# Keys and values by a seven-product (Strassen) form in a two-layer decoder on one core

## The chip, the core and the metric

One core of a Trainium2 chip runs the whole program. Its engines are TensorE (PE: matmuls, with its weight loads beside it), VectorE (DVE), ScalarE (ACT), GpSimd (POOL) and SyncE (SP); each takes its instructions in the order in which they stand in its own queue, and waits at semaphores for the others. Weights come from memory by DMA: SP issues to the hardware queue, POOL to the software queue. A transfer of the software queue can add to what lies at its target ("accumulating transfer"). The metric is the device time of one execution in microseconds, the median of the runs.

## The reference

Two layers over 512 rows of width 1024, in float32. What matters here:

```python
h = rmsnorm(x, norm1_w) * (1 + sc1) + sh1          # sc, sh, g from c @ w_ada
u = h @ w_in                                       # pool, conv, b, c, q, k, v, gate logits
q = apply_partial_rope(rmsnorm(q, q_norm_w), cos, sin)      # by heads of 64; k likewise
o = moba_attention(q, k, v)                        # blocks of 256
merged = (g[0] * (y_pool @ p_pool) + g[1] * (y_conv @ p_conv) + g[2] * (y_attn @ p_attn))
x = x + g1 * (merged @ w_out)
h2 = rmsnorm(x, norm2_w) * (1 + sc2) + sh2
x = x + g2 * ((silu(h2 @ w_gate) * (h2 @ w_up)) @ w_down)
```

`k` and `v` are each 512 columns of `w_in`, so keys and values together are one product of h (512 x 1024) with a 1024 x 1024 matrix.

## The kernel before

Activations lie with features on the 128 partitions: h is eight tiles `big` of 128x512. Every float32 product is made of three (`mm3`): a number is split into a high half, rounded to the matmul's type, and the low half that is left, and high x high, low x high and high x low are added up in PSUM. So all weights need a high half `whi` and a low half `wlo`.

Weights come as a fixed list of chunks, each of eight 128x128 blocks (128x1024, 512 KB). `next_w()` hands out the next chunk and keeps up to four loaded ahead of it. A chunk is fetched by SP into one of three tiles `raw`; `split_w` then writes the high half on ACT (L328) and the low half on DVE (L331), as `raw - whi`. `split_by_transfer` is another way, for the gate columns from 20 on: ACT writes the high half (L339) and its negative into `wlo` (L341), and POOL issues an accumulating transfer that adds the weights on top (L343). There are five tiles each for `whi` and `wlo`.

A Tile scheduler sets the order of instructions, but whatever is wrapped in `pin` or goes through `matmul` stays in the order in which the program names it. Small work on DVE and ACT (pooling steps, convolution, rotary tables, modulation dots) is put on a list `bulk`; each tile of matmuls lets some of it through, at a rate `bulk_rate`, and `flush_bulk()` empties it. Attention runs as a generator (`fibers`) between the matmuls that follow, with a delay counted in the same ticks.

A layer's first part runs so:

1. Eight chunks with four query blocks and three feature columns (the q stage).
2. Feature columns 6, 3 and 7 (24 matmuls of 128x512 each); the pooling chain 0, in layer 0 the rotary tables (`rotary`, L458) and both convolution chains go through `bulk` here.
3. Keys, then values, by `wide()`: 4 chunks of 24 matmuls 128x512 each, for all four groups of 128 rows. Eight dots for the gains G1 (a 512 KB tile of modulation weights each; `ada_dot`, L399) go on here.
4. Feature columns 4 and 5; then, for each of eight output tiles, two gate columns with the pool and conv projections, while attention runs between.
5. GATE2: the attention gates, and the merge of all three branches, whose result `merged` is split again for the output product.

The output product, the second normalisation and the feed-forward follow. Pairs of feed-forward tiles already use a product of seven forms (`GateUp`, `glu_pair`): with halves of the inner dimension and of the rows, the forms are named B21, B11, R1, -V, B22, T3 and T4.

Of the kernel before, what the change touches and what calls it, by code (L numbers as in the profile page):

```python
# [57 lines left out]
NCOL = 74  # L58

# [20 lines left out]
def hybrid_trunk(ctx, tc, xT, ws, ada, cols, pool_w, qk_w, crow, pos, con, out):  # L80
# [210 lines left out]

    def feed_forward():
# [18 lines left out]
    for l in range(L):  # L311
        first_part = [b for b in _plan() if b[0][0] not in ("gate", "up", "down")]
        for blocks in first_part + list(feed_forward()):
            if isinstance(blocks, int):
                pair = GateUp(l, blocks)
                items += [(pair, sub) for sub in range(pair.SUBS)]
            else:
                items.append((None, (l, blocks)))
# [15 lines left out]


# [95 lines left out]
    def ada_step(l, part, j, early):  # L431
        aw = wp.tile([P, D], F32, tag="raw", name=nm("raw"), bufs=RAW) if early else w4([P, D])
        nc.sync.dma_start(aw, ada[l, part, j])
        with tc.issue_after(dots_after[0].ins) if dots_after[0] is not None else nullcontext():
            ins = ada_dot(aw, l, part, j)
        pin(ins)
# [9 lines left out]
    def ada_tasks(l, parts, early=False):  # L446
        out = []
        for part in parts:
            for j in range(KT):
                out.append((1.2, lambda part=part, j=j: ada_step(l, part, j, early)))  # L450
            out.append((0.2, lambda part=part: ada_end(l, part)))
        return out
# [26 lines left out]
    class Norm:  # L479
        def __init__(self, one=False):  # L480
# [7 lines left out]
            self.lo = [bigt() for _ in range(KT)]  # L488

# [43 lines left out]
        def apply(self, l, i, k, lo, hi):  # L533
# [14 lines left out]
            if i == 1:  # L548
                A.activation(self.h[k][:, lo:hi], t[:, lo:hi], AF.Identity, bias=sh)
# [11 lines left out]
        def first_lo(self, k):  # L561
            pin(V.scalar_tensor_tensor(self.lo[k], self.t, mod[0][:, SH1, k:k + 1], f32(self.hi[k]),  # L562
                                       op0=ALU.add, op1=ALU.subtract))

# [42 lines left out]
    def qk_evac(which, qk, ss, t, src):  # L607
        A.activation(qk[t][:, which], src.rearrange("p (h d) -> p h d", d=HD), AF.Copy)
        sq = tmp()
# [221 lines left out]
    for l in range(L):  # L831
# [47 lines left out]
        def wide():  # L879


            pr = ps_pair()
            groups = [ps_mm(), ps_mm(), pr[:, 0], pr[:, 1]]
            for c in range(4):
                w = next_w()
                order = [(kk, t) for kk in range(2) for t in range(TT)]
                for kk, t in sorted(order, key=lambda o: o[1]) if c == 3 else order:
                    k = 2 * c + kk
                    mm3(groups[t], cut(norm.k(k), slice(None), slice(t * P, (t + 1) * P)),
                        wrow(w, 4 * kk), k == 0, k == KT - 1)  # L890
            return groups
# [54 lines left out]

        bulk_rate[0] = 1.4
# [3 lines left out]
        bulk.append((0.4, pool_weights))  # L951
        if l == 0:
            bulk.append((2.0, rotary))
        pool1 = bigt(F32)
        A.activation(pool1, f_ps[1], AF.Copy)
        for j in range(2):
            if j == 1:
                pu = ps_mm()
                feature_tile(pu, next_w())
                uc[1] = bigt(F32)  # L960
# [3 lines left out]
            flush_bulk()  # L964
            z = bigt(F32)
            V.tensor_mul(z, pc, uc[j])
            conv_chain(j, z)
            if j == 1:
                bulk.append((0, lambda: pool_chain(1, pool1)))

        gains = ada_tasks(l, (G1,))
        bulk.extend(gains[:4])
        k_ps = wide()
        for t in range(TT):
            qk_evac(1, qk, ss, t, k_ps[t])
        flush_bulk()
        y_pool, y_conv = [], []
        wc, wsn = rope_tables(l)
        rs = []
        nrq, prq = sm([P, TT, HEADS], tag="nrq", bufs=2), sm([P, TT, HEADS], tag="nrq", bufs=2)  # L980

# [9 lines left out]
        bulk.append((1.6, rstds))  # L991
        for t in range(TT):
# [61 lines left out]
        for step, j in GATE2:  # L1054
# [3 lines left out]
            if j == 0:  # L1058
                drain()
# [327 lines left out]
```

## Time and profile before

| | |
|---|---|
| three runs | 1447.68, 1445.1, 1442.31 us; median 1445.1 |
| profiled execution | 1442.24 us, of which the span of the trace is 1440.5 |
| busy in the span | PE 1433.7, DVE 1014.5, ACT 714.0, POOL 145.7 us |
| moved by DMA | 241.83 MB, mean 168 GB/s |

The times in rows of the profile are microseconds from the start of the span. A row of the timeline has start, duration, engine, line, operation and tiles; square brackets at its end hold idle time of the engine just before it and what ended it. A row of groups has the number of instructions, the total busy time with the mean in nanoseconds of one, and the idle time before. Matmuls are pipelined: each row's duration is longer than the distance to the next one's start.

### The profile page before, as it was taken

What the parts mean: (1) busy time and instruction counts of PE and PEld (TensorE: products, weight loads), DVE (VectorE), ACT (ScalarE), POOL (GpSimd) and SP (SyncE); (2) the same over time, 40 slices, a digit from 0 to 9 for tenths busy, and PEclk for the clock granted to TensorE, in tenths of its full rate; (3) what the DMA queues carried; (4) which work ended last, traced back from release to release, by engine and by line L of the source; (5) the groups of instructions that cost most, each with busy time, mean ns of one, the idle gap of its engine ahead of it and who ended that gap; (6) DMA issues with size and microseconds to landing.
All of it is one profiled execution on the core that took longest, in us unless ns stands there. A gap on an engine that the chain in (4) does not pass through costs nothing.

```text
span 1440.5 us, 21954 instructions
## 1 busy us (share of the span) xinstructions
PE 1433.7 (100%) x8346; PEld 1261.7 (88%) x8346; DVE 1014.5 (70%) x1858; ACT 714.0 (50%) x1199; POOL 145.7 (10%) x204
## 2 busy tenths in 40 slices
PE   9999999999999999999999999999999999999999
PEld 7888888888988998999988888888889989999997
DVE  8887777649686867677798766654578747657663
ACT  5645666733653452535444466666336625525450
POOL 0000110101100311210000000011020102111200
PEclk9999999999999999999999999999999999999999
DMA  9647876665347766756536565567372537637532
GB/s 351 216 149 209 220 184 168 181 229 163 90 140 223 187 179 206 190 146 198 189 125 207 177 146 135 135 154 194 129 208 85 136 114 180 173 105 187 136 88 85
DMA packets 91049, 241.83 MB, mean 168 GB/s; under 512 B 11576, under 2 KB 24256, under 8 KB 90944
## 3 DMA queue, kind: packets, MB, share of 16 engines
q1 hardware_dynamic: 67312, 177.37, 36.8%
q0 software_dynamic: 23040, 62.93, 22.3%
q8 instruction: 65, 1.06, 0.3%
q14 instruction: 40, 0.33, 0.1%
q10 hardware_dynamic: 592, 0.14, 0.0%
HBM read 238.30 MB, written 2.10 MB: 167 GB/s over the span
## 4 chain that ended last, share of the span: by engine, by line
PE 96%; issue 1%; DMA 1%; DVE 1%; ACT 0%; ACTq 0%; DVEq 0%; POOLq 0%
PE mm L151 83%; PE pair L151 12%; PE mm L157 1%; DMA wlo<-in_ws 1%; DMA colt<-in_cols 0%; DVE big L788 0%; DVE big L795 0%; DVE big L562 0%; ACT whi L339 0%; DVE w L399 0%; ACT big L1028 0%; DVE wlo L331 0%; ACT big L575 0%; DVE tmp L555 0%; ACT big L559 0%
## 5 line engine op out<-in xcount | busy, mean ns | idle before, releaser
L151 PE MATMUL mm<-big,whi 128*128 128x512 f32 (+1 forms) x4350 | 1078.0, 339 | 1.0 <-ACT big L1028 1.0
L151 PEld LDWEIGHTS mm<-big,whi 128*128 128x128 f32 x4350 | 744.3, 190 | 87.8 <-issue 2.6
L151 PE MATMUL mm<-big,wlo 128*128 128x512 f32 (+1 forms) x2175 | 735.3, 338 | 0.1
L151 PEld LDWEIGHTS mm<-big,wlo 128*128 128x128 f32 x2175 | 412.6, 190 | 45.3 <-DMA wlo<-in_ws 0.5
L328 ACT ACTIVATE whi<-raw 128x1024 fp32r<-128x1024 f32 (+2 forms) x192 | 198.2, 1034 | 223.2 <-PE mm L151 116.8
L331 DVE TENSOR_TENSOR wlo<-raw,whi 128x1024 fp32r<-128x1024 f32 (+2 forms) x192 | 225.8, 1187 | 53.1 <-ACT whi L328 52.6
L328 ACT ACTIVATE whi<-w 128x1024 fp32r<-128x1024 f32 x72 | 76.2, 1058 | 139.5 <-PE mm L151 85.8
L1073 DVE SCALAR_TENSOR_TENSOR x<-mm,mod,x 128x512 f32<-128x512 f32 (+1 forms) x89 | 61.6, 694 | 75.2 <-PE mm L151 75.0
L399 DVE SCALAR_TENSOR_TENSOR w<-w,csil 128x1024 f32<-128x1024 f32 x80 | 95.9, 1221 | 17.8 <-DMA w<-in_ada 17.7
L331 DVE TENSOR_TENSOR wlo<-w,whi 128x1024 fp32r<-128x1024 f32 x72 | 86.8, 1221 | 28.8 <-ACT whi L328 28.1
L257 POOL DMA_DIRECT2D w<-in_ws x72 | 47.2, 673 | 465.1 <-DVE wlo L331 214.4
L343 POOL DMA_DIRECT2D wlo<-in_ws x48 | 41.0, 855 | 438.1 <-ACT wlo L341 241.5
L259 POOL DMA_DIRECT2D w<-in_ws x72 | 63.4, 906 | 159.0 <-DMA w<-in_ws 155.3
L151 PE MATMUL pair<-whi,big 128*128 128x512 f32 x224 | 76.7, 389 | 0.0
L339 ACT ACTIVATE whi<-raw 128x1024 fp32r<-128x1024 f32 x48 | 51.0, 1063 | 49.4 <-PE mm L151 32.1
L151 PE MATMUL pair<-big,whi 128*128 128x256 f32 (+1 forms) x376 | 74.0, 294 | 0.0
L151 PEld LDWEIGHTS pair<-big,whi 128*128 128x128 f32 x376 | 60.4, 191 | 2.2
L151 PE MATMUL mm<-whi,big 128*128 128x512 f32 x160 | 56.9, 392 | 0.6 <-ACT big L559 0.4
L1033 DVE SCALAR_TENSOR_TENSOR big<-big,mm 128x512 f32<-128x512 f32 x48 | 32.8, 684 | 33.1 <-PE mm L151 31.8
L151 PE MATMUL pair<-big,wlo 128*128 128x256 f32 (+1 forms) x188 | 55.3, 294 | 0.0
L341 ACT ACTIVATE wlo<-whi 128x1024 fp32r<-128x1024 f32 x48 | 50.8, 1059 | 0.3
L151 PEld LDWEIGHTS pair<-whi,big 128*128 128x128 f32 x224 | 42.1, 188 | 8.6
(212 smaller groups left out, 1349.3 us busy)
## 6 DMA issues: line engine op xcount, KB each, us to landing
raw<-in_ws SPq DMA_DIRECT2D x146, 512.0 KB, 4.4
w<-in_ada SPq DMA_DIRECT2D x80, 512.0 KB, 5.5
w<-in_ws POOLq DMA_DIRECT2D x144, 256.0 KB, 4.7
wlo<-in_ws POOLq DMA_DIRECT2D x48, 512.0 KB, 6.8
raw<-in_ws SPq DMA_DIRECT2D x64, 256.0 KB, 4.1
raw<-in_ws SPq DMA_DIRECT2D x24, 384.0 KB, 3.6
raw<-in_ada SPq DMA_DIRECT2D x16, 512.0 KB, 4.4
raw<-in_ws SPq DMA_DIRECT2D x16, 448.0 KB, 5.5
```

Of the source, the lines that this page charges most:

```text
L151: tc.keep_in_program_order(T.matmul(*a, **k))
L157: tc.keep_in_program_order(T.transpose(*a))
L257: nc.gpsimd.dma_start(dst, self.source(0, 1))
L259: nc.gpsimd.dma_start(dst, self.source(*other), accum_op=ALU.add)
L328: A.activation(hi[:, :n], raw[:, :n], AF.Copy)
L331: ins = V.tensor_sub(lo[:, :n], raw[:, :n], f32(hi)[:, :n])
L339: A.activation(hi[:, :n], raw[:, :n], AF.Copy)
L341: A.activation(lo[:, :n], f32(hi)[:, :n], AF.Copy, scale=-1.0)
L343: nc.gpsimd.dma_start(lo[:, i:i + m].rearrange("p b n -> p (b n)"), src, accum_op=ALU.add)
L399: return V.scalar_tensor_tensor(aw, aw, 1.0, csil, op0=ALU.mult, op1=ALU.mult, accum_out=mod[l][:, part, j:j + 1])
L1033: V.scalar_tensor_tensor(sg, sg, 1.0, branch, op0=ALU.add, op1=ALU.mult)
L1073: V.scalar_tensor_tensor(x[k][:, lo:hi], src, mod[l][:, part, k:k + 1], x[k][:, lo:hi], op0=ALU.mult, op1=ALU.add)
```

## The change

Keys and values become one product with seven forms, in both layers. The weights' quarters are named by `(kk, z)`, with `kk` the half of the inner dimension and `z` 0 for the keys, 1 for the values: B11 and B21 are the two halves for the keys, B12 and B22 those for the values. The rows of h are halved too (`early`, `late`: rows 0-255 and 256-511). A class `KeyValue` makes 14 chunks (7 forms, 2 chunks each):

- chunks 0 to 3 (B21, B11) are fetched raw; their low halves come by accumulating transfer;
- chunks 4 to 9 come from two tiles `x`: POOL copies one quarter into each and adds another by accumulating transfer, ahead of time; DVE adds a raw quarter of 128x1024 between the forms, and `split_w` makes the halves;
- chunks 10 and 11 come from four tiles of 128x512 (`far`), filled in the same way by POOL (`summed_rows`) and split row by row (`split_rows`);
- chunks 12 and 13 are fetched raw and split by ACT and DVE.

On the side of h, `sums_one` and `sums_two` make the sums of row halves on DVE and split them; the first norm keeps eight whole tiles `h` for this. Keys and values are put together from the PSUM groups with copies on ACT and additions on DVE. Each chunk now serves 12 matmuls of 128x512: 168 in a layer where there were 192.

Also moved: `rotary()` from the `bulk` list to right behind the q stage; the convolution chains, the second pooling chain and the pooling weights to behind the values, where three gate columns now stand first (the list of chunks is reordered by `AFTER_KEYS`); the eight G1 dots from the K/V stage to GATE2; the loads for layer 0's SC2/SH2 dots run one ahead of their dots.

```diff
+KEYS = 12
+AFTER_KEYS = (20, 28, 21, 4, 5, 29)
...
+        def summed(self, tile, other, cp):
+            flat = tile.rearrange("p b n -> p (b n)")
+            nc.gpsimd.dma_start(flat, self.source(0, 1, cp))
+            nc.gpsimd.dma_start(flat, self.source(other[0], other[1], cp), accum_op=ALU.add)
...
+        def load(self, sub):
+            form, cp = divmod(sub, 2)
+            if sub == 0:
+                self.near, self.far = [None] * 2, [None] * 2
+            if sub == 2:
+                self.x = [w4([P, C_BLOCKS, P]) for _ in range(2)]
+                for i in range(2):
+                    self.summed(self.x[i], (1, 1), i)
+            if form < 2:
+                kk = 1 - form
+                raw = self.raw(kk, 0, cp)
+                if form == 1:
+                    self.near[cp] = raw
+                return split_by_transfer(raw, self.l, self.blocks(kk, 0, cp))
+            if form in (2, 3):
+                w = split_w(self.x[cp], C_BLOCKS)
+                pin(V.tensor_add(self.x[cp], self.x[cp], self.near[cp]))
+                if form == 2:
+                    self.near[cp] = self.raw(1, 0, cp)
+                    self.far[cp] = [bigt(F32) for _ in range(2)]
+                    self.summed_rows(self.far[cp], (0, 0), cp)
+                return w
+            if form == 4:
+                return split_w(self.x[cp], C_BLOCKS)
+            if form == 5:
+                return split_rows(self.far[cp])
+            return split_w(self.raw(1, 1, cp), C_BLOCKS)
...
+        def keys_values(qk, ss, made, tables, then):
...
+            for _ in form(e, "B21", True):
+                pass
+            for _ in form(a, "B11", True):
+                pass
+            for t in range(2):
+                A.activation(qk[t][:, 1], heads(a[t]), AF.Copy)
+                V.tensor_add(qk[t][:, 1], qk[t][:, 1], heads(e[t]))
+                squares(1, ss, t, qk[t][:, 1].rearrange("p h d -> p (h d)"))
+            for cp in form(c, "R1", True):
+                two[cp] = sums_two(cp, *made[cp][:2])
...
+            for cp in form(a, "-V", False):
...
+            for _ in form(c, "B22", False):
...
+            for _ in form(a, "T3", False):
...
+            for cp in form(d, "T4", True):
...
+        if l == 0:
+            rotary()
         bulk_rate[0] = 1.4
         pool_chain(0, f_ps[0])
...
-        if l == 0:
-            bulk.append((2.0, rotary))
...
-        gains = ada_tasks(l, (G1,))
-        bulk.extend(gains[:4])
-        k_ps = wide()
...
-        fibers.append([3, attention(l, qk, v, nrq, prq, y_attn)])
+        fibers.append([5, attention(l, qk, v, nrq, prq, y_attn)])
+        bulk.append((0.4, pool_weights))
+        for j in range(2):
+            conv_chain(j, zs[j])
+        pool_chain(1, pool1)
+        bulk_rate[0] = 1.6
+        ready = [gate() for _ in range(3)]
+        flush_bulk()
...
             if j == 0:
                 drain()
+                late = len(bulk)
+                bulk.extendleft(reversed(ada_tasks(l, (G1,))))
+                bulk_rate[0] = 1.3
```

The order of instructions at the places that the prediction speaks of follows. A row has the line, the operation, output and inputs, and the shape. First VectorE in layer 0, behind the q stage, before: the low half `wlo_592` is that of feature column 7, `wlo_598` and `wlo_604` are those of the first two chunks of the keys; L915 to L925 are the pooling chain.

```order
L331 TENSOR_TENSOR wlo_592<-raw_588,whi_590 128x1024
L915 COPY big_618<-big_581 128x1
L920 TENSOR_TENSOR big_618<-big_581 128x511
L331 TENSOR_TENSOR wlo_598<-raw_594,whi_596 128x1024
L331 TENSOR_TENSOR wlo_604<-raw_600,whi_602 128x1024
L915 COPY big_621<-big_618 128x2
L917 SCALAR_TENSOR_TENSOR big_621<-big_618,cont 128x510
L925 SCALAR_TENSOR_TENSOR tmp_624<-big_621,cont,big_581 128x496
```

The same engine and place, now: `wlo_634` is the low half of column 7; `rope`, `cosc` are the rotary table, L984 to L990 the sums of h's row halves, and L670 their low halves.

```order
L986 SCALAR_TENSOR_TENSOR big_728<-big_729,big_150 128x256
L565 SCALAR_TENSOR_TENSOR rope_615<-rope_612,ang 128x32
L990 SCALAR_TENSOR_TENSOR big_729<-big_728,big_154 128x256
L566 SCALAR_TENSOR_TENSOR rope_615<-rope_612,rope_615 128x32
L567 SCALAR_TENSOR_TENSOR rope_615<-rope_612,rope_615 128x32
L670 TENSOR_TENSOR big_734<-big_728,big_733 128x512
L568 TENSOR_SCALAR rope_615<-rope_615 128x32
L984 TENSOR_TENSOR big_738<-big_155,big_151 128x256
L569 TENSOR_SCALAR rope_615<-rope_615 128x32
L985 TENSOR_TENSOR big_737<-big_151 128x256
L572 COPY cosc<-cosc 128x4x8
L402 TENSOR_TENSOR wlo_634<-raw_630,whi_632 128x1024
```

The low half of column 7 stood ahead of most of the pooling chain and of all of the rotary table, and stands behind both now; the first keys' low halves are gone from this engine.

ScalarE at this place, before: `whi_596`, `whi_602` and `whi_685` are high halves of the keys' first chunks, L572 a high half of the pooling result, L475 the table and the sine.

```order
L328 ACTIVATE whi_596<-raw_594 128x1024
L328 ACTIVATE whi_602<-raw_600 128x1024
L328 ACTIVATE whi_685<-raw_683 128x1024
L572 ACTIVATE big_628<-tmp_624 128x512
L941 ACTIVATE big_701<-big_680,colt 128x512
L328 ACTIVATE whi_722<-raw_720 128x1024
L961 ACTIVATE big_717<-mm_682 128x512
L903 ACTIVATE pwh_650<-tmp_644 128x256
L475 ACT_TABLE_LOAD
L475 ACTIVATE sins<-rope_661 128x4x8
```

And now: `whi_638`, `whi_645`, `whi_699` are the high halves of the keys' first three chunks (L419), L421 the negative copies that the accumulating transfers wait for, L669 high halves of the pooling result and of the sums of h.

```order
L419 ACTIVATE whi_638<-raw_636 128x1024
L419 ACTIVATE whi_645<-raw_643 128x1024
L669 ACTIVATE big_672<-tmp_668 128x512
L571 ACT_TABLE_LOAD
L571 ACTIVATE sins<-rope_604 128x4x8
L419 ACTIVATE whi_699<-raw_697 128x1024
L669 ACTIVATE big_733<-big_728 128x512
L571 ACTIVATE cosc<-rope_615 128x4x8
L421 ACTIVATE wlo_640<-whi_638 128x1024
L421 ACTIVATE wlo_647<-whi_645 128x1024
L421 ACTIVATE wlo_701<-whi_699 128x1024
```

The cosine stands ahead of the first negative copy, and the third high half, with its transfer, ahead of the cosine. On POOL the transfers of this place are, in a row (before, the queue held the pooling weights' clearing and then the gates' low halves):

```order
L314 DMA w_691<-in_ws 128x1024
L314 DMA w_692<-in_ws 128x1024
L315 DMA w_691<-in_ws 128x1024
L315 DMA w_692<-in_ws 128x1024
L423 DMA wlo_640<-in_ws 128x1024
L423 DMA wlo_647<-in_ws 128x1024
L423 DMA wlo_701<-in_ws 128x1024
L423 DMA wlo_753<-in_ws 128x1024
L353 DMA big_821<-in_ws 128x512
L353 DMA big_822<-in_ws 128x512
```

The copies for `x` and what is added to them go first, the four low halves of the first forms next, then the rows for T3.

Last, VectorE in GATE2 of layer 0, before: L1033 and L1067 merge a tile, L573 is its low half, L399 are modulation dots.

```order
L1033 SCALAR_TENSOR_TENSOR big_3161<-big_3161,mm_3291 128x512
L1067 TENSOR_TENSOR big_3161<-big_3161,big_2430 128x512
L1033 SCALAR_TENSOR_TENSOR big_3194<-big_3194,mm_3310 128x512
L1067 TENSOR_TENSOR big_3194<-big_3194,big_2612 128x512
L573 TENSOR_TENSOR big_3307<-big_3161,big_3306 128x512
L573 TENSOR_TENSOR big_3326<-big_3194,big_3325 128x512
L331 TENSOR_TENSOR wlo_3368<-raw_3364,whi_3366 128x1024
L331 TENSOR_TENSOR wlo_3374<-raw_3370,whi_3372 128x1024
L399 SCALAR_TENSOR_TENSOR w_3382,mod_116<-w_3382,csil 128x1024
```

And now the corresponding stretch (L1202 and L1241 merge, L670 is the low half, L479 are dots), a little ahead of the last tiles:

```order
L479 SCALAR_TENSOR_TENSOR w_3236,mod_116<-w_3236,csil 128x1024
L479 SCALAR_TENSOR_TENSOR w_3251,mod_116<-w_3251,csil 128x1024
L402 TENSOR_TENSOR wlo_3267<-raw_3263,whi_3265 128x1024
L479 SCALAR_TENSOR_TENSOR w_3275,mod_116<-w_3275,csil 128x1024
L479 SCALAR_TENSOR_TENSOR w_3290,mod_116<-w_3290,csil 128x1024
L402 TENSOR_TENSOR wlo_3305<-raw_3301,whi_3303 128x1024
L479 SCALAR_TENSOR_TENSOR w_3314,mod_116<-w_3314,csil 128x1024
L1202 SCALAR_TENSOR_TENSOR big_2997<-big_2997,mm_3307 128x512
L1241 TENSOR_TENSOR big_2997<-big_2997,big_1715 128x512
L670 TENSOR_TENSOR big_3326<-big_2997,big_3325 128x512
L479 SCALAR_TENSOR_TENSOR w_3336,mod_116<-w_3336,csil 128x1024
L1202 SCALAR_TENSOR_TENSOR big_3055<-big_3055,mm_3329 128x512
```

Dots that stood behind the merged tiles, or in the K/V stage, stand between them.

More of the change, by code (lines that the diff above doesn't have):

```diff
@@ L290, in load, with __init__, blocks, source @@
             return split_w(raw, C_BLOCKS)
+    class KeyValue:
+        SUBS = 14
+        def __init__(self, l):
+            self.l = l
+        def blocks(self, kk, z, cp):
+            return [("in", kk * HK + 2 * cp + i, KEYS + 4 * z + b) for i in range(2) for b in range(4)]
+        def source(self, kk, z, cp):
+            (_, _, src), = runs(self.l, self.blocks(kk, z, cp))
+            return src
+        def begin(self):
+            pass
[3 more added lines that the diff above has]
+            nc.gpsimd.dma_start(flat, self.source(other[0], other[1], cp), accum_op=ALU.add)
+        def raw(self, kk, z, cp):
+            raw = rawt()
+            fetch(raw, self.l, self.blocks(kk, z, cp))
+            return raw
+        def load(self, sub):
[25 more added lines that the diff above has]
+            return split_w(self.raw(1, 1, cp), C_BLOCKS)
+        def summed_rows(self, tiles, other, cp):
+            for i, tile in enumerate(tiles):
+                c = slice(i * S, (i + 1) * S)
+                nc.gpsimd.dma_start(tile, self.source(0, 1, cp)[:, c])
+                nc.gpsimd.dma_start(tile, self.source(other[0], other[1], cp)[:, c], accum_op=ALU.add)
     def feed_forward():
@@ L332, in split_w, with split_rows @@
         pin(ins)
+        return hi, lo
+    def split_rows(tiles):
+        hi = wp.tile([P, C_BLOCKS, P], F32R, tag="whi", name=nm("whi"), bufs=5)
+        lo = wp.tile([P, C_BLOCKS, P], F32R, tag="wlo", name=nm("wlo"), bufs=5)
+        rows = lambda t, i: t[:, 4 * i:4 * i + 4].rearrange("p b n -> p (b n)")
+        for i, tile in enumerate(tiles):
+            A.activation(rows(hi, i), tile, AF.Copy)
+            pin(V.tensor_sub(rows(lo, i), tile, f32(rows(hi, i))))
         return hi, lo
@@ L446, in ada_tasks, with step @@
     def ada_tasks(l, parts, early=False):
[L447 to L451, printed above, removed]
+        every = [(part, j) for part in parts for j in range(KT)]
+        kept, out = [], []
+        load = lambda n: ada_load(l, *every[n], early, kept)
+        def step(n):
+            if early and n + 1 < len(every):
+                load(n + 1)
+            if not early:
+                load(n)
+            ada_step(l, *every[n], kept)
+        if early:
+            out.append((1.2, lambda: load(0)))
+        for n, (part, j) in enumerate(every):
+            out.append((1.2, lambda n=n: step(n)))
+            if j == KT - 1:
+                out.append((0.2, lambda part=part: ada_end(l, part)))
         return out
@@ L877, in feature_tile, with sums_one @@
                 mm3(o, wblk(w, k), norm.k(k), k == 0, k == KT - 1)
[L879 to L891, printed above, removed]
+        def sums_one(c):
+            h1, h2 = norm.h[c], norm.h[HK + c]
+            one, two = bigt(F32), bigt(F32)
+            r1, nv, t3 = one[:, :BLOCK], one[:, BLOCK:], two[:, :BLOCK]
+            V.tensor_sub(t3, h2[:, BLOCK:], h1[:, BLOCK:])
+            V.tensor_sub(r1, h1[:, :BLOCK], h1[:, BLOCK:])
+            V.scalar_tensor_tensor(nv, t3, -1.0, h1[:, :BLOCK], op0=ALU.mult, op1=ALU.subtract)
+            return one, two, split_from(one)
@@ L1036, in hybrid_trunk @@
         for j in range(KT):
-            s0, s1 = gate(), gate()
+            s0, s1 = [ready.pop(0) if ready else gate() for _ in range(2)]
+            if j == 2:
+                bulk_rate[0] = 0.35
             if j % 2 == 0:
```

129 lines of the change are left out of this document (96 added, 33 removed).

## The prediction

> **What bounds the kernel now.** I read the engine shares first, then the clock slices, the waits of TensorE and the chain that ended last. From the page, and from the waits of TensorE:
>
> ```profile
> span 1440.5 us, 21954 instructions
> PE 1433.7 (100%) x8346; PEld 1261.7 (88%) x8346; DVE 1014.5 (70%) x1858; ACT 714.0 (50%) x1199; POOL 145.7 (10%) x204
> PEclk9999999999999999999999999999999999999999
> ...
> PE pair L151 <- POOL ones L203: 1.1, 1, 1.1
> PE mm L151 <- ACT big L1028: 1.0, 2, 0.5
> PE mm L151 <- ACT big L559: 0.4, 1, 0.4
> PE pair L151 <- ACT ccol L773: 0.3, 1, 0.3
> PE pair L151 <- DVE big L795: 0.2, 1, 0.2
> ```
>
> TensorE (PE) is busy for 1433.7 of 1440.5 us, at a granted clock of 0.9 or more in every slice, and its five waits add up to 3.0 us. The time is the number of matmuls times their pitch. So a removed matmul is paid back in full, unless a wait stands where it stood, and since there are next to no waits now, every wait that the change makes is a loss. The question is therefore whether VectorE (DVE), ScalarE (ACT) and the transfers keep ahead of the shortened products. The pitch, from the chain (start, duration, number), and the place where the keys begin in layer 0, from the timeline (the last matmul of feature column 7 has the weights second, the first of the keys has them first):
>
> ```profile
> 53.76 19.72 PE mm L151 x87
> ...
> 71.73 0.39 PE L151 MATMUL mm<-big,wlo 128*128 128x512 f32 x1
> 71.95 0.39 PE L151 MATMUL mm<-whi,big 128*128 128x512 f32 x1
> ```
>
> 19.72 / 87 = 0.2267 us for a 128x512 matmul. Each lasts 0.39 us but the next starts 0.22 us later, so the pitch, not the duration, is the price. Call T0 = 71.95 the start of the keys; column 7 is 24 matmuls, 5.44 us, and begins at 66.51.
>
> **The matmuls removed.** Keys and values were 8 weight chunks of 24 matmuls in each layer, 192; now they are 14 of 12, 168, all 128x512. 24 x 0.2267 = 5.44 us a layer, 10.88 us in both. The stage shrinks from 43.5 to 38.1 us, and a chunk is used up in 2.72 us instead of 5.44. This is the gain if nothing waits.
>
> **The work that must hide in the stage.** Windows, one for each row: the last columns ahead of the keys and the keys and values, in layer 0 and in layer 1; then, for comparison, one pair of feed-forward tiles, which already uses this kind of product.
>
> ```profile
> 53.80:72.00 18.20, 18.20 (x82) 15.06 (x81) 14.58 (x28) 11.92 (x19) 0.31 (x1) 1.00 0.72 239
> 72.00:115.50 43.50, 43.50 (x194) 36.02 (x193) 35.95 (x90) 17.78 (x26) 1.84 (x2) 1.00 0.51 169
> 763.60:782.00 18.40, 18.40 (x83) 15.24 (x82) 13.36 (x24) 9.31 (x16) 0.31 (x1) 1.00 0.68 214
> 782.00:825.50 43.50, 43.50 (x193) 36.02 (x193) 34.34 (x76) 17.31 (x24) 1.69 (x2) 1.00 0.53 165
> 480.00:497.00 17.00, 17.00 (x144) 17.00 (x143) 14.05 (x20) 9.94 (x16) 5.75 (x9) 1.00 0.87 219
> ...
> q1 hardware_dynamic: 67312, 177.37, 36.8%
> q0 software_dynamic: 23040, 62.93, 22.3%
> ...
> L331 DVE TENSOR_TENSOR wlo<-raw,whi 128x1024 fp32r<-128x1024 f32 (+2 forms) x192 | 225.8, 1187 | 53.1 <-ACT whi L328 52.6
> L399 DVE SCALAR_TENSOR_TENSOR w<-w,csil 128x1024 f32<-128x1024 f32 x80 | 95.9, 1221 | 17.8 <-DMA w<-in_ada 17.7
> L1033 DVE SCALAR_TENSOR_TENSOR big<-big,mm 128x512 f32<-128x512 f32 x48 | 32.8, 684 | 33.1 <-PE mm L151 31.8
> ...
> 67.35 1.53 DVE L943 SCALAR_TENSOR_TENSOR big<-big,colt,big 128x511 f32<-128x511 f32 x2
> 69.94 0.42 DVE L904 TENSOR_TENSOR pwl<-tmp,pwh 128x256 fp32r<-128x256 f32 x1
> ```
>
> Columns after the window are the length, the busy time of PE, weight loads, DVE, ACT and POOL, the clock, the DMA share and GB/s. DVE is busy 35.95 of 43.5 us in the K/V stage of layer 0. The change takes from there the eight gain dots (8 x 1.22 = 9.8 us, row of L399) and the rest of the pooling, convolution and rotary chains (two convolutions of 1.53, some ten steps of about 0.7: 10 us, an estimate), and adds: ten subtractions for low halves of 128x1024 where there were eight (+2.4 us), four additions of 128x1024 (4.9), eight evacuation additions of 512 (5.5), and of the rows' 16 sums of 256 and 8 low halves of 512 about half, the rest lying ahead of the keys (8 x 0.42 + 6 x 0.69 = 7.5). That comes to 36.5 us in 38.1: tight, but the feed-forward window shows DVE at 14.05 of 17 and ACT at 9.94 with PE busy for all of it. I charge nothing inside the stage. ACT gains 8 copies of h a layer in the normalisation ahead (8 x 0.61, the row of L572 below), and evacuations and negative copies in the stage; at 17.78 of 43.5 it covers them. Without that cover each late low half would stop PE for what it is late, up to 1.2 us.
>
> The transfers: a layer's keys and values now fetch 20 pieces of 512 KB where there were 8: 8 by the hardware queue, 12 by the software queue (4 low halves, 8 for two-term sums). The queues' shares above give their rates with all 16 engines at work: 177.37 MB in 0.368 x 1440.5 us is 335 GB/s, 62.93 MB in 0.223 x 1440.5 is 196 GB/s. 8 x 0.524 MB / 335 + 12 x 0.524 / 196 = 12.5 + 32.1 = 44.6 us. That is more than the 38.1 us of the stage, so it must start ahead of it, and it does: the copies for the sums stand behind the last scale and shift dots, which free their tiles (near 47 us, row below), some 25 us ahead of T0.
>
> **Layer 0, just ahead of the keys.** Here the change moves work into a place without slack. Rows of DVE, ACT and the software queue's low halves (L343: what it takes to issue, and how long until it has landed):
>
> ```profile
> 46.82 1.22 DVE L399 SCALAR_TENSOR_TENSOR w<-w,csil 128x1024 f32<-128x1024 f32 x1
> 57.68 1.22 DVE L331 TENSOR_TENSOR wlo<-raw,whi 128x1024 fp32r<-128x1024 f32 x1
> 63.40 1.06 ACT L328 ACTIVATE whi<-raw 128x1024 fp32r<-128x1024 f32 x1 [3.00 <-DMA raw<-in_ws]
> 64.36 0.61 ACT L572 ACTIVATE big<-tmp 128x512 fp32r<-128x512 f32 x1
> 65.01 0.69 DVE L573 TENSOR_TENSOR big<-tmp,big 128x512 fp32r<-128x512 f32 x1 [1.36 <-ACT big L572]
> 68.81 1.28 ACT L475 ACT_TABLE_LOAD   x1
> ...
> L343 POOL DMA_DIRECT2D wlo<-in_ws x48: 835/855/987, 107.3 to 1004.2; - x48
> DMA to landing us min/median/max: 5.2/6.8/11.3
> L341 ACT ACTIVATE wlo<-whi 128x1024 fp32r<-128x1024 f32 x48 | 50.8, 1059 | 0.3
> ```
>
> Column 7's low half is made at 57.68 now, 9 us ahead of its first use (66.51 plus two matmuls, 66.96). In the new order it stands behind the whole rotary table, whose last step waits for ACT; ACT stands there behind the high halves of the keys, and the third of these behind its transfer. That transfer takes the place of the one which ended ACT's idle time at 63.40. Walk: the pooling result and the Sin table load (0.61 and 1.28) keep ACT until about 64.4; high half 1.06, row's high half 0.61, DVE's 0.69, two 256-wide sums (about 0.4 each), the last rotary steps and ACT's cosine (some 0.8 together), then 1.22 for column 7: about 69. PE wants it at 66.96, so it waits 2.0 us. Bounds: 0 if DVE and ACT run a little denser than I walk; 4 if the raw transfers, which the new copies now meet in a stretch that moves 239 GB/s, land 2 us late.
>
> Next in line are the four low halves by transfer. ACT writes the first negative copy (1.06) only behind the cosine, about 67.9 to 69.0; then POOL issues and the data land 6.8 us later (median), 75.8. PE starts the keys at 71.95 + 2.0 and wants it one matmul later, 74.2: 1.6, bounds 0 (landing 5.2) and 5.7 (11.3). I take 1.4, since the wait for column 7 is itself rounded up. The next three come 2.7 us apart at the software queue's 196 GB/s, as fast as PE uses them, so I charge them nothing; 2 us if the hardware queue takes half the engines meanwhile.
>
> A rule of the Trainium skill speaks for less here: "DMA: Bandwidth & Descriptors", section "Anatomy of one DMA — SWDGE (gpsimd) path", fits a transfer of that path as 2.0 us plus the bytes at 436 GB/s, so an estimate of 3.2 us for 512 KB. By it the first low half would be there at about 72.2, the 1.4 us would go and the sum below would be 1437.1. The row's shortest landing, 5.2 us, says that an accumulating transfer amid other traffic is not that fast, so I keep the row.
>
> In layer 1 there is no rotary table and the same four transfers can be issued from about 763, as ACT has 9.31 of 18.4 us busy there: no charge, bound 2 us.
>
> **The first tiles behind the values.** Two convolution chains, the pooling chain and the pooling weights move behind the values; three gate tiles (16.3 us of PE) are placed there to cover them, and their first reader comes behind those and two more columns: nothing, with 1 us as the bound, as POOL's queue now also holds the weights' clearing behind the last transfer.
>
> **The end of the gates.** The gain dots move into the stage where attention's gated sums are merged. Windows of layer 0, and what ends that stage (the last two merged low halves, and PE's first matmul of the output product that is near them):
>
> ```profile
> 302.00:318.00 16.00, 16.00 (x72) 13.27 (x71) 8.64 (x12) 5.30 (x7) 0.00 (x0) 1.00 0.60 212
> 318.00:334.00 16.00, 16.00 (x73) 13.24 (x72) 11.22 (x16) 6.09 (x8) 0.00 (x0) 1.00 0.16 58
> 336.05 1.37 DVE L573 TENSOR_TENSOR big<-big,big 128x512 fp32r<-128x512 f32 x2
> 339.17 0.62 PE L151 MATMUL mm<-big,whi 128*128 128x512 f32 x2
> ```
>
> DVE's 8.64 + 11.22 = 19.9 of 32 us become 29.6 with eight dots, and some layer 0 modulation dots remain besides. The last merged row is ready at 337.4 now and wanted at about 339.2; two or three dots stand ahead of it that were behind it, so it comes near 340: 0.9 us in layer 0, bounds 0 and 2. Layer 1 has no such remaining dots: nothing.
>
> **Sum.** -10.9 + 2.0 + 1.4 + 0.9 = -6.6 us. The profiled execution took 1442.24 us (span 1440.5 and 1.7 around it), 2.9 below the median 1445.1 of the three runs; from it the sum gives 1435.6, from the median 1438.5, and the median is what I forecast against. Half a per cent, about what a measurement of this kernel can tell from no change, is 7.2 us: the line to faster is 1437.9, next to the forecast.
>
> **Rivals.**
> Clean: every wait above is inside my rounding, 10.9 us come through, less at most 1.5: 1434.2 to 1435.7. For it: PE waits only 3.0 us in a kernel whose feed-forward already runs such products without a gap. Against it: 9 us of lead for column 7 is given up in the new order.
>
> Slow train: the four transfers of layer 0 land late and spaced by more than 2.72 us. 5.7 instead of 1.4 for the first and 2 for the others make 6.3 more, half of it 3.2: a net gain of 0.3 to 3.4, so 1441.5 to 1445. For it: the longest landing is 11.3 us. Against it: the median is 6.8.
>
> Slower: the transfers bound both K/V stages. What must arrive by a stage's end is 12.5 us by the hardware queue, 6.3 us for the four weight chunks ahead (4 x 0.524 MB / 335), and 6.29 MB by the software queue, in 38.1 + 25 = 63 us. It breaks the cover when the software queue gets less than 6.29 MB / 44.2 us = 142 GB/s, and eats the whole 5.44 us of a layer below 6.29 / 49.6 = 127 GB/s; at 110 GB/s it loses 13 us a layer, which gives 1445.1 - 10.9 + 26 = 1460. For it: 196 GB/s holds only with the engines to itself. Against it: the feed-forward window moves 219 GB/s by both queues with PE busy throughout.
>
> A rule bears on this: the Trainium skill, same page, section "SWDGE vs HWDGE vs iDMA", says that each engine takes the two paths' queues in turn. That would share, not starve; no run here shows it alone.
>
> **How the numbers follow.** Forecast with waits of 4 us, by one and a half more or less (1436 to 1441): 0.50. Clean: 0.22. Slow train: 0.20. Slower or nearly so (1446 to 1460): 0.08. Faster by over 0.5% is the clean case and a bit under half of the forecast's: 0.45. Slower by over 0.5% is the larger part of the last: 0.05. The rest is the same, 0.50. The range leaves out the last rival and reaches from the clean end to the slow train's: 1433.8 to 1445.5.
>
> **What would show it.** Right: matmuls fall by 48 and their 128x512 pitch stays 0.227; two waits of PE in layer 0, one for column 7's low half near 67 us (by DVE), one for a low half by transfer near 74; layer 1's stage without a wait; DVE near full at the stage where the gains now stand. Wrong: a low half made ahead of 67 us (clean); waits for low halves by transfer in layer 1 too, with landings over 10 us (the rivals with the transfers); or PE waiting for DVE within the stage, which would make DVE, that I cost at nothing there, the bound.

## The result, and the profile after

The changed kernel takes 1458.9 us (median of four runs, 1456.9 to 1460.6) against 1443.8 for the kernel before in the same set: a ratio of 1.010, interval 1.0074 to 1.0126. I forecast 6.6 us less; it is 15 more. From the page of the changed kernel, then TensorE's waits (engine, line, releaser: us in total, times, longest):

```profile
span 1458.9 us, 22095 instructions
PE 1433.4 (98%) x8298; PEld 1254.5 (86%) x8298; DVE 1056.0 (72%) x1938; ACT 757.0 (52%) x1266; POOL 171.4 (12%) x236
PEclk9999999998999999999999999999999999999999
...
PE mm L155 <- DVE wlo L402: 4.3, 1, 4.3
PE mm L155 <- ACT big L669: 3.5, 4, 1.3
PE pair L155 <- DMA wlo<-in_ws: 3.2, 1, 3.2
PE mm L155 <- DMA wlo<-in_ws: 2.9, 2, 1.7
PE mm L155 <- ACT big L844: 1.4, 1, 1.4
PE mm L161 <- DVE big L1202: 1.4, 1, 1.4
```

48 matmuls are gone, yet PE's busy time is what it was (1433.7), and the waits, 3.0 us before, are now over 20. Busy time that should have fallen by 10.9 us points to slower matmuls: one slice of the clock row is an 8, and 13.7 us in two stretches are at half clock, which costs up to 6.8 us. The places come out of one landmark, the same run of 288 matmuls in each layer's feed-forward, in the chain that ended last, before and after (start, duration, number):

```profile
427.08 49.95 PE mm L151 x288
1138.15 49.95 PE mm L151 x288
```

```profile
444.23 49.95 PE mm L155 x288
1156.65 49.95 PE mm L155 x288
```

Layer 0 arrives there 17.15 us late and layer 1 adds 1.35. Since each should have come 5.44 earlier, layer 0 loses 22.6 us and layer 1 6.8, 29.4 in all. Windows of the changed kernel (length, busy time of PE, PEld, DVE, ACT, POOL, then clock, DMA share, GB/s), and layer 0's column 7:

```profile
66.00:72.00 6.00, 1.68 (x7) 1.06 (x7) 5.96 (x21) 4.58 (x7) 0.49 (x1) 1.00 0.26 87
72.10:75.40 3.30, 3.30 (x10) 2.53 (x9) 2.29 (x8) 3.30 (x6) 1.98 (x3) 0.50 0.76 182
340.00:355.00 15.00, 10.79 (x31) 5.92 (x31) 11.77 (x19) 6.53 (x8) 0.00 (x0) 0.78 0.44 144
348.60:358.70 10.10, 7.71 (x16) 4.53 (x16) 8.29 (x12) 4.75 (x6) 0.00 (x0) 0.50 0.49 160
...
71.66 0.51 PE L155 MATMUL mm<-big,wlo 128*128 128x512 f32 x1 [4.32 <-DVE wlo L402]
```

Three losses are large. At the front TensorE waits 4.3 us for column 7's low half and then runs 3.4 us at a granted clock of 0.50, which costs 1.7 more; the keys begin at 78.4 instead of 71.95. At the end of the gates it waits in pieces from 341 to 354, and from 348.5 to 358.7 runs at half clock: 10 us in all, by the distances between matmul starts. In layer 1 it waits 3.2 us for a key's low half and 1.7 for a gate's. Some 6 us of layer 0 are small waits beside attention and at the first gate.

What came as predicted: the keys' and values' stage itself, 38.1 us in layer 0 from its first matmul to its last without a wait, and the pitch.

### The profile page after: what moved, and what is told of

Same layout as the page of the kernel before. It is cut to its first block, busy times and chain, and to the rows that moved or that the text cites. A ratio compares the mean times of both kernels' runs of the same rounds, so it can differ in the third digit from the quotient of the medians.

```text
span 1458.9 us, 22095 instructions
## 1 busy us (share of the span) xinstructions
PE 1433.4 (98%) x8298; PEld 1254.5 (86%) x8298; DVE 1056.0 (72%) x1938; ACT 757.0 (52%) x1266; POOL 171.4 (12%) x236
## 4 chain that ended last, share of the span: by engine, by line
PE 82%; DVE 6%; DMA 6%; ACT 3%; issue 2%; POOL 0%; SPq 0%; ACTq 0%; POOLq 0%; DVEq 0%
PE mm L155 72%; PE pair L155 9%; DMA raw<-in_ws 4%; DMA wlo<-in_ws 2%; PE mm L161 1%; DVE w L479 1%; DVE wlo L402 1%; ACT whi L399 1%; ACT whi L419 1%; DMA x<-in_xT 0%; DVE tmp L651 0%; DVE big L658 0%; DVE raw L479 0%; DVE big L1202 0%; ACT big L669 0%
## 5 line engine op out<-in xcount | busy, mean ns | idle before, releaser
L399 ACT ACTIVATE whi<-raw 128x1024 fp32r<-128x1024 f32 (+2 forms) x180 | 185.1, 1029 | 200.5 <-PE mm L155 103.6
L402 DVE TENSOR_TENSOR wlo<-raw,whi 128x1024 fp32r<-128x1024 f32 (+2 forms) x180 | 211.4, 1184 | 45.0 <-ACT whi L399 44.7
L399 ACT ACTIVATE whi<-w 128x1024 fp32r<-128x1024 f32 x84 | 88.9, 1058 | 156.8 <-PE mm L155 91.9
L402 DVE TENSOR_TENSOR wlo<-w,whi 128x1024 fp32r<-128x1024 f32 x84 | 101.2, 1220 | 33.8 <-ACT whi L399 33.1
L423 POOL DMA_DIRECT2D wlo<-in_ws x56 | 49.5, 887 | 497.7 <-ACT wlo L421 174.0
L479 DVE SCALAR_TENSOR_TENSOR w<-w,csil 128x1024 f32<-128x1024 f32 x80 | 95.7, 1220 | 13.3 <-DMA w<-in_ada 13.1
L419 ACT ACTIVATE whi<-raw 128x1024 fp32r<-128x1024 f32 x56 | 59.5, 1063 | 50.2 <-PE mm L155 35.1
L155 PE MATMUL pair<-whi,big 128*128 128x512 f32 x256 | 83.0, 389 | 0.0
L421 ACT ACTIVATE wlo<-whi 128x1024 fp32r<-128x1024 f32 x56 | 59.1, 1059 | 0.5
L155 PE MATMUL pair<-wlo,big 128*128 128x512 f32 x128 | 50.1, 391 | 3.2 <-DMA wlo<-in_ws 3.2
L670 DVE TENSOR_TENSOR big<-tmp,big 128x512 fp32r<-128x512 f32 x48 | 33.0, 691 | 25.3 <-ACT big L669 24.3
```

Of the source, the lines that this page charges most:

```text
L155: tc.keep_in_program_order(T.matmul(*a, **k))
L399: A.activation(hi[:, :n], raw[:, :n], AF.Copy)
L402: ins = V.tensor_sub(lo[:, :n], raw[:, :n], f32(hi)[:, :n])
L419: A.activation(hi[:, :n], raw[:, :n], AF.Copy)
L421: A.activation(lo[:, :n], f32(hi)[:, :n], AF.Copy, scale=-1.0)
L423: nc.gpsimd.dma_start(lo[:, i:i + m].rearrange("p b n -> p (b n)"), src, accum_op=ALU.add)
```

## The experiments

Ratios are to the kernel before, with a 95% interval. What an edit gains or loses is told against the changed kernel.

**Rotary back on the list.** 1455.3 us, 1.0084 (1.0068 to 1.0101).

```diff
-        if l == 0:
-            rotary()
...
+        if l == 0:
+            bulk.append((2.0, rotary))
```

> The changed kernel with the rotary tables back on the list of small work, where they stood before, so that the low half of feature column 7 stands ahead of them again. Theory A (the waits are separate, each made by an order of instructions): the 4.3 us wait of TensorE near 67 us goes, and with it the half-clock stretch of 3.4 us behind it; 6.5 us less than the changed kernel, 1452.4, or 1454 if the first low half by transfer is then late. Rival B (the transfers as a whole are the bound): the wait comes back at the next late weight; 1457 to 1459.

The wait near 67 us and the half clock behind it are gone from the trace, and the layer 0 landmark comes at 437.28, 7.0 us earlier. Layer 1 gives 0.7 back: its wait for a key's low half grows from 3.2 to 4.2 us, and this time 3.4 us at half clock follow. Theory A holds at the front. The profiled executions differ by 6.3 us and the medians by 3.6; executions of both kernels spread over some 4 us, so I read the place from the traces and the size from both. The median lies between what theory A (1452 to 1454) and rival B (1457 to 1459) forecast.

**SC2/SH2 dots as before the change.** 1459.5 us, 1.0118 (1.0094 to 1.0142): no gain.

```diff
-            if early and n + 1 < len(every):
-                load(n + 1)
-            if not early:
-                load(n)
+            load(n)
...
-        bulk_rate[0] = 0.0
+        bulk_rate[0] = 0.27
```

> The changed kernel with layer 0's SC2/SH2 dots as before: no load one ahead, rate 0.27 from the first gate on. The eight gain dots stay at the end of the gates. Theory A1 (weights are late there because modulation loads hold raw tiles and stand ahead of them in SP's queue): the waits of 341 to 354 us and the 10 us at half clock shrink by half or more, 1449 to 1454. Rival A2 (the dots' time on VectorE is the cause): unchanged, 1457 to 1460. Rival B: unchanged as well.

The time says the rival and the trace says A1: the loss at the end of the gates falls from 10 us to 2.5, but a dot without its load ahead now holds VectorE for 4.1 us, and attention and TensorE (3.3 us at 218 us, with half clock) behind it. One edit mended a wait and made another.

**Gain dots ahead of SC2/SH2, in the gates.** 1481.8 us, 1.0261 (1.024 to 1.0281).

```diff
-                bulk.extendleft(reversed(ada_tasks(l, (G1,))))
-                bulk_rate[0] = 1.3
...
+        bulk.extend(ada_tasks(l, (G1,)))
         if l == 0:
             bulk.extend(ada_tasks(l, (SC2, SH2), True))
-        bulk_rate[0] = 0.0
+        bulk_rate[0] = 0.45
```

> The changed kernel with the eight gain dots ahead of the SC2/SH2 dots in the gate columns (rate 0.45 from the first gate on), none of them at the end of the gates. SC2/SH2 come later for it and still hold raw tiles there. Theory A2 (VectorE's 9.8 us of gain dots make the end of the gates late): 8 to 10 us less, 1449 to 1451, unless attention is now late. Rival A1 (raw tiles and SP's queue): 0 to 3 us less, 1456 to 1459.

A clear miss for A2. Beside attention, at that rate, the dots make new waits in both layers (5.7 us at 901 alone), and the end of the gates, free of gain dots, still loses 10 us to late SC2/SH2 dots. So the gain dots are not what that end waits for. The time is outside both forecasts.

**Tiles x asked for earlier.** 1452.8 us, 1.0065 (1.005 to 1.008): the best single edit that leaves no work out.

```diff
         def begin(self):
-            pass
+            self.x = [w4([P, C_BLOCKS, P]) for _ in range(2)]
+            for i in range(2):
+                self.summed(self.x[i], (1, 1), i)
```

> The changed kernel with the transfers for the two-term tiles x asked for four chunks earlier, so that in layer 1 POOL issues them ahead of all four low halves and not between them. Theory A (POOL waits in its queue for a copy to land, with the low halves behind it): layer 1's 3.2 us wait near 810 us goes, 1455 to 1456; layer 0 as before. Rival B: the wait stays or moves to the next form; 1458 to 1460.

POOL's queue in layer 1, from the timeline, in the changed kernel and then here:

```profile
781.20 0.86 POOL L423 DMA_DIRECT2D wlo<-in_ws  x1 [106.75 <-PE pair L155]
783.01 0.57 POOL L314 DMA_DIRECT2D w<-in_ws  x1 [0.95 <-issue]
791.52 0.85 POOL L315 DMA_DIRECT2D w<-in_ws  x1 [7.95 <-DMA w<-in_ws]
792.07 1.20 POOL L423 DMA_DIRECT2D wlo<-in_ws  x1
...
801.49 0.86 POOL L315 DMA_DIRECT2D w<-in_ws  x1 [6.79 <-DMA w<-in_ws]
802.03 1.20 POOL L423 DMA_DIRECT2D wlo<-in_ws  x1
```

```profile
779.31 0.86 POOL L421 DMA_DIRECT2D wlo<-in_ws  x1 [47.93 <-ACT wlo L419]
784.75 0.86 POOL L421 DMA_DIRECT2D wlo<-in_ws  x1 [4.58 <-ACT wlo L419]
787.17 0.86 POOL L421 DMA_DIRECT2D wlo<-in_ws  x1 [1.56 <-ACT wlo L419]
791.86 0.86 POOL L421 DMA_DIRECT2D wlo<-in_ws  x1 [3.83 <-ACT wlo L419]
```

In the changed kernel POOL stood 7.95 and 6.79 us until a copy had landed, since the transfer that adds to it is next in its queue, with the keys' low halves behind. With the tiles asked for earlier, the fourth low half goes out at 791.9 instead of 802.0, and TensorE no longer waits for it. Layer 0, which I had expected as before, comes 4.3 us earlier as well (landmark 439.95). Its second raw tile of the keys takes 4.7 us now instead of 10.1, and still column 7 waits 3.3 us: another raw transfer, at 50.1 us beside the copies for x, takes 5.9 us and holds ScalarE up.

**SC2/SH2 dots begun at the first gate.** 1455.1 us, 1.0088 (1.0072 to 1.0103).

```diff
-        bulk_rate[0] = 0.0
+        bulk_rate[0] = 0.35
...
-            if j == 2:
-                bulk_rate[0] = 0.35
```

> The changed kernel with layer 0's SC2/SH2 dots at rate 0.35 from the first gate on instead of from the third output tile, the load one ahead kept, so that all sixteen stand ahead of the gain dots, which stay at the end of the gates. If late SC2/SH2 dots with their raw tiles make the end of the gates wait: 6 to 8 us less than the changed kernel, 1451 to 1453. If the eight gain dots by themselves do: 1456 to 1460.

```profile
340.00:355.00 15.00, 14.58 (x64) 11.62 (x63) 14.70 (x22) 6.02 (x8) 0.00 (x0) 1.00 0.46 152
PE pair L155 <- DMA wlo<-in_ws: 5.5, 2, 5.2
```

The window of the end of the gates holds 64 matmuls now, against 31, at full clock, with the eight gain dots still there: the loss of 10 us is 0.8. That settles that the late SC2/SH2 dots are the cause. How they act is read from the chain of the changed kernel: a late dot ends and frees its raw tile, only then is an output weight loaded into it, and the merged tile's high half (L669) stands behind that weight's (L399) on ScalarE.

```profile
338.51 0.68 DVE raw L479
339.67 4.33 DMA raw<-in_ws
344.11 1.06 ACT whi L399
345.17 0.53 ACT big L669
```

No run separates these dots' raw tiles from their time on VectorE. The saving in the median is less than that, because the dots that now stand beside the first attention tiles cost some 4 us there, and layer 1's wait for a low half became 5.2 us, with half clock.

**Rotary ahead, in the kernel before.** 1443.5 us against 1442.3, 1.0006 (0.9997 to 1.0015): no difference that can be told.

```diff
+        if l == 0:
+            rotary()
         bulk_rate[0] = 1.4
...
-        if l == 0:
-            bulk.append((2.0, rotary))
```

> The kernel before with one part of the change alone: rotary tables right behind the q stage, ahead of the low half of column 7; keys and values as before, no transfers for sums. If the order alone makes the wait, TensorE stands 4 us near 67 us and then runs at half clock for 3.4 us: 1448 to 1449. If the raw transfer that took 10 us beside the copies for x has its part in it, the wait is 1 to 2.5 us without half clock: 1444 to 1446. If the new order costs nothing without the new products: 1442 to 1443.

```profile
PE mm L151 <- DVE wlo L331: 0.4, 1, 0.4
```

The order that I named as the cause is there, and TensorE waits 0.4 us. So the rotary table's place alone is not enough. The sums of h's row halves, which share that stretch of VectorE in the changed kernel, are not in this run; the next one has them.

**No transfers for x** (their part of keys and values is left out). 1449.9 us, 1.0049 (1.0034 to 1.0064).

```diff
-            nc.gpsimd.dma_start(flat, self.source(0, 1, cp))
-            nc.gpsimd.dma_start(flat, self.source(other[0], other[1], cp), accum_op=ALU.add)
+            nc.gpsimd.memset(flat, 0.0)
```

> The changed kernel without the copies and accumulating transfers into the two tiles x of a layer (they are set to zero by POOL instead; their part of keys and values is left out). The orders on VectorE and ScalarE stay. If these transfers make the raw one at the front take 10 us, it lands within 5 to 6, column 7's low half comes some 3 us earlier, and the wait near 67 us is 1 to 2 us with no half clock; layer 1's wait for a low half behind them on POOL goes too: 1448 to 1452. If the order alone makes them, the front's wait stays over 3.5 us and only layer 1's goes: 1454 to 1456.

ScalarE's second high half of the keys, in the changed kernel and then without the transfers; and two waits of TensorE without them:

```profile
63.93 1.06 ACT L419 ACTIVATE whi<-raw 128x1024 fp32r<-128x1024 f32 x1 [2.48 <-DMA raw<-in_ws]
```

```profile
58.60 2.07 ACT L418 ACTIVATE whi<-raw 128x1024 fp32r<-128x1024 f32 x2
PE mm L155 <- DVE wlo L401: 0.6, 1, 0.6
PE pair L155 <- ACT big L668: 1.8, 1, 1.8
```

Without the copies for x, both raw tiles are there when ScalarE comes to them at 58.6; with them the second is had at 63.9, as its transfer takes 10.1 us in the chain (53.73 to 63.85). The wait for column 7 falls from 4.3 to 0.6 us, and with the rotary table back on the list and the transfers kept it is gone too: this wait needs the order and the shared transfers together. The 10.1 us are not the only way that the transfers act, as the run with tiles x earlier shows. Then the first matmuls with a key's low half wait 1.8 us at 73 (the profile names ScalarE; that low half's transfer went out at 67.7 and landed 7.4 us later, at 75.1, when the wait ended), the term that I had put at 1.4. From 75.5 on 3.4 us at half clock follow, so the front still loses some 4.6 us of its 6.4; most of this run's gain, 5.0 us, is in layer 1.

**Three mended together** (rotary, tiles x, rate 0.35). 1441.5 us against 1442.3, 0.9996 (0.9987 to 1.0005).

> Three of the orders mended together in the changed kernel: rotary tables back on the list of small work, transfers for the tiles x asked for four chunks earlier, SC2/SH2 dots at rate 0.35 from the first gate on (the load one ahead stays). Theory A (separate waits): the front's 6.2 us, some 6 us in layer 1 and some 7 us at the end of the gates all go: 1439 to 1441, faster than the kernel before (1442.7). Rival B (the transfers bound it): no more than the best single one, 1448 to 1453. In between, 1442 to 1447, some waits moved.

The waits named so far are gone, and 17.4 us with them, of the 21 that they made together (6.2, 10 and 4.9); that speaks against one bound by transfers. But the landmark of layer 0 comes at 430.47 where 421.64 would be the full saving: 8.8 us stay lost there, nearly all between the values and the output product, and 2.0 in layer 1.

**Dots spread, or begun later.** The three with rate 0.46 and no burst: 1442.4 us, 1.000 (0.999 to 1.001). From the second output tile at 0.52: 1456.5, 1.0104 (1.0086 to 1.0122).

```diff
-        bulk_rate[0] = 0.0
+        bulk_rate[0], credit[0] = 0.46, -1.0
```

> The three mended orders with the SC2/SH2 dots spread evenly: rate 0.46 from the first gate and the credit that lets three dots through at once taken away. If that burst on VectorE makes the 5 us of waits between 128 and 200 us: 1437 to 1439, faster than the kernel before (1442.3). If attention there is late for another reason: 1440 to 1442, as with the three alone.

> As the last, but the dots begin at the second output tile with rate 0.52, so that the first attention tiles are free of them. If they disturb attention wherever they stand: 1437 to 1440, a little better than the even spread; if their density is what counts: 1440 to 1443.

The even spread takes away the waits from 128 to 200 us and puts others from 200 to 340; denser, attention waits up to 3.5 us at a time. The even spread came within 0.4 us of its second forecast, the same as the three alone; the later start missed both of its own. So neither the burst nor the early tiles make the loss; dots per stretch are what is left, and the next runs bear on it.

**No SC2/SH2 dots in layer 0, or sparse ones.** Left out: 1436.5 us, 0.9956 (0.9941 to 0.997). At 0.27: 1448.1, 1.0035 (1.0021 to 1.0049).

> The three mended orders, with layer 0's sixteen SC2/SH2 dots and their loads left out (both parts are set to zero and their bias added). What is left of the loss stands between the values and the second normalisation of layer 0, 7 to 8 us. If these dots crowd attention on VectorE there: 6 to 8 us less than with them, 1433 to 1436, the full saving of the product. If the convolution, pooling and gain work moved there does it: 1439 to 1442.

> The three mended orders with the SC2/SH2 dots at the kernel before's density, rate 0.27 from the first gate, no burst; nine stand ahead of the gain dots, seven behind them. If the density of dots among the attention work costs most and a late dot with its raw tile little: 1437 to 1440. If late dots hold raw tiles while the output product needs them, as in the changed kernel: 1445 to 1450.

Without the dots TensorE loses hardly more from 160 to 300 us than in the kernel before (3.2 us against 3.0, by the distances between matmul starts). The time is still only 5.8 of the 10.9 us better, and just outside the forecast: in the profiled execution a wait of 1.9 us for a low half at the first gate, with half clock behind it, costs 3.8 us. At the old density, too, the stretch from 128 to 318 us loses hardly more than before (3.8 us against 3.1), but the seven dots left over come with their raw tiles to the output product, and 12 us are lost there, with 13.7 us at half clock. In the kernel before sixteen dots fitted at that rate; three gate tiles fewer stand behind their start now, and seven don't.

**Dots divided.** SC2 in the gates at 0.27, SH2 with tiles of its own in the output product; G2 behind the second normalisation (first), or left in the output product (second, whose edit is shown).

```diff
-            bulk.extend(ada_tasks(l, (SC2, SH2), True))
-        bulk_rate[0] = 0.0
+            bulk.extend(ada_tasks(l, (SC2,), True))
+        bulk_rate[0], credit[0] = 0.27, -1.0
...
-        bulk.extend(ada_tasks(l, (G2,)))
+        bulk.extend(ada_tasks(l, (SH2, G2) if l == 0 else (G2,)))
```

> The three mended orders, with layer 0's dots divided: SC2 in the gate columns at the kernel before's rate of 0.27, SH2 in the output product with tiles of its own, G2 behind the second normalisation. All dots are computed. If only the number of dots beside attention and late raw tiles cost the rest, both are gone: 1435 to 1438, faster than the kernel before by 5 us. If SH2's dots now make the second normalisation late: 1440 to 1444.

> As the last, but G2's dots stay in the output product behind those of SH2, so sixteen dots stand beside it on VectorE, in some 40 us. If VectorE has room there: the same as the last, 1435 to 1438. If it hasn't: waits at the second normalisation, 1440 to 1446.

With G2 moved: 1445.1 us, 1.0021 (1.001 to 1.0033), outside both forecasts; nothing is lost up to the normalisation, but in the feed-forward a weight's transfer takes 8.8 us beside the loads of G2's dots (a wait of 3.8 us at 445, and half clock). With G2 left: 1435.9 us, 0.9956 (0.9944 to 0.9969), faster than both kernels, with every dot computed. Its landmarks and its waits:

```profile
423.92 49.95 PE mm L155 x288
1130.99 49.95 PE mm L155 x288
...
PE pair L155 <- POOL ones L207: 1.1, 1, 1.1
PE mm L155 <- ACT big L1171: 1.0, 2, 0.5
PE mm L155 <- DVE big L1200: 0.6, 1, 0.6
```

Layer 0 is 3.2 us ahead of the kernel before and layer 1 adds 4.0: 7.2 of the 10.9 us.

## Why the prediction was wrong

- The gain, 48 matmuls at 0.2267 us, was right, and so was, in layer 0, that nothing waits inside the stage; in layer 1 the 3.2 us below stand inside it.
- "19.72 / 87 ... So a removed matmul is paid back in full, unless a wait stands where it stood": right, but each wait was priced at its own length. A wait of a few us can also halve the granted clock for 3.4 us or a multiple of it. This term was missing from the sum; in the profiled run of the changed kernel it is 1.7 us at the front and about 5 at the end of the gates. The Trainium skill has it, in "TensorE: Matmul & The Clock Gate", section "Part 1: The HAM clock gate (the "warmup" mystery)": half rate after about 3.4 us of idling, full rate after as long a busy stretch. I weighed another rule and left this one out, which spoke against the change; the traces agree with the length of the half-rate stretch (3.41 us or a whole multiple), but not with so long an idling: here 1.9 us were enough (the run without dots, 111 us).
- Column 7: 2.0 us, measured 4.3 and 1.7 of clock. Place and order were right. The steps of the walk, as they are listed, add up to 69.6 and not 69, so 2.6 us. The walk took the third raw transfer from the time of the kernel before; it was the second that came late, 10.1 us beside the copies for x, which held ScalarE up for 2.5 us. I named that as a bound of 2 us and did not take it.
- The first low half: 1.4 us, measured 0, since column 7's wait hid it. In the run without the transfers for x, where column 7 hardly waits, it shows as 1.8: the two terms cover each other in part, and were added. How far is not fixed: with the gain dots in the gates, 3.5 and 1.4 us stood one behind the other. (The upper bound of 5.7 was a slip: 11.3 us of landing instead of 6.8 make 6.1.)
- Layer 1, "no charge": measured 3.2 there and 1.7 at the gate. I had shown POOL's order for layer 0 alone; in layer 1 the copies and the low halves alternate, and one waits for the other. What I costed was the transfers' rate, not the queue in which they stand.
- The end of the gates: 0.9 us, measured 10. I counted VectorE's dots. The gain dots were harmless; late loads with raw tiles took the output weights' places, by the chain shown above. Their later start, in the diff a rate of 0 up to the third output tile, did that, and my working has no term for it.
- "Nothing, with 1 us as the bound" for what moved behind the values: some 6 us, as small waits beside attention, most likely because the same dots had fewer matmuls to hide behind: without the SC2/SH2 dots the stretch loses hardly more than before.
- The rival that ended slower, transfers that bound both stages, was not it: mending queues and orders gave back 17.4 us of the 21 that the waits made.

What stays open: 3.7 us of the saving in the best version, of which the traces show 0.5 to 1.4 us at a time beside attention and at the second normalisation, and not one cause.

## What to carry to other kernels

Where one engine is always busy, a change that saves its work is worth what the feeding engines' orders leave of it: walk every queue, the DMA issuers' too and in each layer, and count tiles that a moved load holds and not only the engine time of what uses it. Price a wait of the matmul engine at its length, and add 1.7 us for a stretch at half clock where more than about half of a 3.4 us stretch would be idle (the next section has the numbers). When several waits come at once, mend them together before judging one, since a mended one moves the others.

## What the runs showed of the hardware

How long a wait must be before the clock falls is not one number. A wait of 4.3 us (changed kernel, 67 us) was followed by 3.4 us at half clock, one of 3.2 (the same, layer 1) was not; with the tiles x asked for earlier, 3.3 us were enough, and with the gain dots in the gates, 3.5 us at the same place were not. With three mended, 1.5 us were enough at 157 us, in a stretch of small transposes. Windows, first of the gain dots in the gates behind their wait of 3.5 us, then of three mended behind its wait of 1.5:

```profile
71.00:75.00 4.00, 4.00 (x19) 3.24 (x18) 2.84 (x8) 4.00 (x7) 2.10 (x3) 1.00 0.81 179
```

```profile
159.40:162.60 3.20, 3.20 (x9) 2.46 (x8) 2.74 (x6) 3.20 (x9) 0.86 (x1) 0.50 0.50 165
```

That fits windows of fixed places in time, 3.41 us each, that count work and not a single gap. In every trace with several stretches at half clock, these start a whole number of 3.413 us apart (in the changed kernel at 72.02 and 348.50, 81 times). With such windows laid over all sixteen traces, each window at full clock in which TensorE was idle for 1.82 us or more is followed by half clock; with less idle time only three are followed by it (1.56, 1.58 and 1.69 us). The windows that end where the half clock begins in the changed kernel and in the run without the transfers for x, and the two that share the wait of 3.5 us in the run with the gain dots in the gates:

```profile
68.61:72.02 3.41, 0.36 (x2) 0.31 (x3) 3.38 (x11) 2.14 (x4) 0.51 (x1) 1.00 0.00 0
72.12:75.53 3.41, 1.57 (x7) 1.03 (x6) 2.49 (x6) 2.30 (x4) 3.02 (x5) 1.00 1.06 204
65.58:68.99 3.41, 1.61 (x8) 0.99 (x6) 3.38 (x16) 2.07 (x4) 0.00 (x0) 1.00 0.31 117
68.99:72.40 3.41, 1.70 (x7) 1.42 (x8) 2.73 (x8) 3.33 (x5) 1.71 (x2) 1.00 0.22 41
```

TensorE is idle there for 3.05, 1.84, 1.80 and 1.71 us, and only the first two are followed by half clock. That a window counts work, and where its threshold lies, is my reading of these lengths.

A copy of 512 KB on POOL's queue kept what adds to it, and all behind that, 6.8 and 8.0 us waiting in layer 1. And the same copies made a plain transfer of 512 KB take 10.1 us, where the median of its kind is 4.3.
